# A decoder layer on one core: half two of the tokens first in the output projection, S1 products early, sums of h by token tile

## The chip, the cores and the metric

The kernel runs on one core of a Trainium2 chip. Its engines are TensorE (PE, with its weight loads shown apart as PEld), VectorE (DVE), ScalarE (ACT), GpSimd (POOL) and SyncE (SP), which issues the DMAs. The metric is the device time of one execution, in microseconds.

## The reference

One hybrid decoder layer in float32, 1024 tokens of 1024 channels. The part around the change is its end:

```python
x = x + gate1 * jnp.dot(merged, w_out)                    # output projection
h2 = _rmsnorm(x, norm2_w) * (1.0 + scale2) + shift2
ffn = jnp.dot(jax.nn.silu(jnp.dot(h2, w_ffn_gate)) * jnp.dot(h2, w_ffn_up), w_ffn_down)
x = x + gate2 * ffn                                       # w_ffn_gate, w_ffn_up: 1024 x 2816
```

## The kernel before, in words

Every large product is made in three parts: each factor is split into hi (rounded to fp32r by ACT) and lo (the rest, a subtraction on DVE or POOL), and PE adds hi·hi, hi·lo and lo·hi in one PSUM bank. A 128x512 output block of depth 512 so takes twelve matmuls.

**Output projection** (L1258 to L1315). It runs in two passes over the eight token tiles of 128 tokens, one for each half of the output channels. A tile takes 24 matmuls of 512 columns. In the second pass each tile is then finished: addition to x (L1283), sum of squares (L1284), reciprocal root on POOL (L183), two scalings to `xn` (L1296), eight transposes on PE (L1299), and eight scale-and-shift operations from PSUM to `hraw`, four on ACT (L1305) and four on DVE (L1307). The first matmul of a tile is kept behind the transposes of a tile two or three earlier by an order constraint without a wait (`turns_first`).

**Feed-forward, gate and up.** h is cut in four blocks of 512 channels by 512 tokens: h11 and h21 are the two channel halves of token half one (tiles 0 to 3), h12 and h22 those of half two (tiles 4 to 7). The products follow Winograd's form of Strassen: 256 output columns of one weight matrix (a `Stream`, 22 in all: gate and up for 11 column blocks p) need seven products M1 to M7 of a weight factor by a block or sum of h: M1 with h11, M2 with h21, M4 with h22, M5 with S1 = h12 + h22, M6 with S2 = S1 - h11, M7 with S3 = h11 - h12, M3 with S4 = h21 - S2. The weight factors of M5, M6, M7 and M4 are differences of weight blocks (L743, L747). M1, M6, M7, M4 add up in one bank A (tag `ya`, four buffers), M5 and M3 in B (tag `yb`, two).

Weights come in as `raws`, four buffers of 512 KB, two to a stream; a factor goes through `tmp` (four buffers) to a slot `fhi`/`flo` (five), hi on ACT (L710), lo on POOL (L711).

Before the change the early products are M1 and M2 of streams 0 to 3 (p = 0, 1), 96 matmuls, as they need half one alone, whose split blocks h11 and h21 are put together tile by tile (L1220, L1221, lo on POOL). After the last tile come the sums S1, S2, S3, S4 (four operations of 128x512 each, L1415) and their splits (L1422 on ACT, L1423 on DVE), and with them the remaining five products of the first two streams; then the streams follow one after the other, a factor prepared two products ahead (`run`, `behind`). Split blocks live in seven slabs (`COMBOS`), which are shared with the buffers of the output projection.

The order in which an engine gets its instructions is set when the kernel is compiled, by a scheduler that follows dependencies and priorities; it moves instructions ahead of others of the same engine where they are ready sooner.

Of the kernel before, what the change touches and what calls it, by code (L numbers as in the profile page):

```python
# [43 lines left out]
def tile_hybrid_layer(ctx: ExitStack, tc: tile.TileContext, x, c, w_ada, b_ada, norm1_w, w_in,  # L44
# [659 lines left out]
    EARLY = ["M1", "M2"]  # L704

# [3 lines left out]
    def split_block(src, hi, lo):  # L709
        nc.scalar.activation(hi, src, AF.Copy)  # L710
        nc.gpsimd.tensor_sub(lo, src, f32(hi))  # L711

    class Stream:


        def __init__(self, env, w, c0):
            self.env, self.w, self.c0 = env, w, c0
            self.c, self.ready, self.blocks = {}, {}, {}
            self.early = False
            self.next = None  # L720
# [11 lines left out]
        def prepare(self, m):  # L732
            if m not in self.ready:
                self.open()
                self.ready[m] = self.factor(m)

        def factor(self, m):
# [3 lines left out]
            elif m == "M4":  # L741
                src = self.t2
                nc.vector.tensor_sub(src, b["21"], src)  # L743
            else:
                src = four(self.env.tmp())
                x, y = {"M5": ("12", "11"), "M6": ("22", None), "M7": ("22", "12")}[m]
                nc.vector.tensor_sub(src, b[x], b[y] if y else self.t1)  # L747
# [5 lines left out]
            split_block(src, hi, lo)  # L753
            return hi, lo

        def copy(self, c, ps):
            self.c[c] = self.env.quad(self, c)
            nc.scalar.activation(self.c[c], ps, AF.Copy)
# [4 lines left out]
        def product(self, m, after=None):  # L763
# [3 lines left out]
            hhi, hlo = self.env.side[SIDE[m]]  # L767
            if m == "M1":
                self.A = self.env.a()
            if m == "M5":  # L770
                self.B = self.env.b()
            ps = self.B if m in ("M5", "M3") else self.env.b() if m == "M2" else self.A
            for k in range(4):
                first, last = k == 0 and m in ("M1", "M5", "M2"), k == 3
                mm = nc.tensor.matmul(ps, lhsT=whi[:, k, :], rhs=hhi[:, k, :], start=first, stop=False,  # L775
# [3 lines left out]
                nc.tensor.matmul(ps, lhsT=wlo[:, k, :], rhs=hhi[:, k, :], start=False, stop=last,  # L779
# [7 lines left out]
            if m == "M6":  # L787
                self.copy("12", ps)
            if m == "M3":
# [3 lines left out]
            if m == "M2" and self.early:  # L793
                self.m2 = self.env.quad(self, "m2")
                nc.scalar.activation(self.m2, ps, AF.Copy)
                return
# [19 lines left out]
    class GateEnv:  # L816
        n_q, n_raw = 0, 0

# [371 lines left out]
    COMBOS = {"h11": 3, "h21": 4, "S1": 1, "S2": 0, "h22": 6, "S4": 2, "S3": 5}  # L1190
# [27 lines left out]
    def put_combo(name, o, src):  # L1218
        hi, lo = (c[:, :, o:o + P] for c in combo[name])
        nc.scalar.activation(hi, src, AF.Copy)  # L1220
        nc.gpsimd.tensor_sub(lo, src, f32(hi))  # L1221
# [10 lines left out]

    early_w = {}
    turned = {}
# [5 lines left out]
    early_raw = {}  # L1240

    def early_load(p):
        for u, w in enumerate((w_ffn_gate, w_ffn_up)):
            raw = early_raw[p, u] = raw_pair().rearrange("p (k n) -> p k n", k=KT)
            nc.sync.dma_start(out=raw, in_=w[:, 2 * p * P:(2 * p + 1) * P].rearrange("(k p) n -> p k n", p=P))

    def early_split(p, slots):
        for i, m in enumerate(("M1", "M2")):
            for u in range(2):
                hi, lo = slots(2 * u + i)  # L1250
                split_block(early_raw[p, u][:, 4 * i:4 * i + 4, :], hi, lo)
                early_w[p, u, m] = hi, lo

    def slab_slots(p):
        t = slab_tile((0, 6)[p], [P, 4, 2, H], R, "early")
        return lambda i: (four(t[:, i, 0, :]), four(t[:, i, 1, :]))

    for hf in range(2):  # L1258
# [15 lines left out]
        for t in range(NT):  # L1274
# [16 lines left out]
            if t == 0:  # L1291
                for name in ("h11", "h21"):
                    alloc_combo(name)
            for g in range(2):
# [5 lines left out]
                for i in range(4):  # L1300
# [7 lines left out]
            if th == 0:  # L1308
                put_combo("h11", o, hraw[0][:, 0, :, o:o + P])
                put_combo("h21", o, hraw[0][:, 1, :, o:o + P])  # L1310
            if t == 4:
                early_load(0)
                early_split(0, slab_slots(0))
            if t == 5:
                early_load(1)  # L1315
                early_split(1, slab_slots(1))
# [13 lines left out]
    class FfnEnv:  # L1330
        def __init__(self):
# [5 lines left out]
        def quad(self, st, c):  # L1337
            if st.p < 2 and c == "11":
                return held[:, 2 * st.p + st.u, :]
            if st.p == 1 and c == "m2":  # L1340
# [3 lines left out]
        def use(self, st, c):  # L1344
            if st.u == 0:
                src = st.A if c == "21" else st.c[c]
                if c == "21":
                    st.c[c] = quad_tile("c21")
                nc.scalar.activation(st.c[c], src, AF.Silu)
            else:  # L1350
                a = streams[st.p, 0].c[c]
                nc.vector.tensor_mul(a, a, st.A if c == "21" else st.c[c])
# [58 lines left out]
    def sums(a, b, op):  # L1411
        out = []
        for k in range(4):
            out.append(quad_tile("hs"))
            nc.vector.tensor_tensor(out[k], a[k], b[k], op=op)  # L1415
        return out

    def split_combo(name, srcs, eng):
        alloc_combo(name)
        for k in range(4):  # L1420
            hi, lo = (c[:, k, :] for c in combo[name])
            nc.scalar.activation(hi, srcs[k], AF.Copy)  # L1422
            eng.tensor_sub(lo, srcs[k], f32(hi))  # L1423

    held = ffn.tile([P, 4, H], F32, name="held", tag="dw")
    held2 = const.tile([P, 2, H], F32, name="held2", tag="gate")
    streams = {}
    for p in range(NP):
        for u, w in enumerate((w_ffn_gate, w_ffn_up)):
            st = streams[p, u] = Stream(fenv, w, 2 * p * P)  # L1430
            st.p, st.u = p, u
            st.ready = {m: early_w[p, u, m] for m in EARLY if (p, u, m) in early_w}
            st.early = p < 2
    turns = {(0, 0, "M1"): {0: 6}, (0, 1, "M1"): {2: 7}}
    for p in range(2):
        for m in EARLY:
            for u in range(2):
                streams[p, u].product(m, turns.get((p, u, m)))
    h11, h21, h12, h22 = ([hr[:, g, k, :] for k in range(4)] for hr in hraw for g in range(2))
    s1 = sums(h12, h22, ALU.add)  # L1440
    split_combo("S1", s1, nc.vector)
    s2 = sums(s1, h11, ALU.subtract)
    split_combo("S2", s2, nc.vector)
    for p in range(2):
        for u in range(2):
            streams[p, u].add("11", streams[p, u].m2)
    s3 = sums(h11, h12, ALU.subtract)
    s4 = sums(h21, s2, ALU.subtract)
    split_combo("S4", s4, nc.vector)
    split_combo("h22", h22, nc.vector)  # L1450
    split_combo("S3", s3, nc.vector)
    flow = [streams[p, u] for p in range(NP) for u in range(2)]
    flow[0].open()
    flow[1].open()
    seq = [(st, m) for m in ORDER if m not in EARLY for st in flow[:2]]
    seq += [(st, m) for st in flow[2:] for m in ORDER if not (st.early and m in EARLY)]

# [198 lines left out]
```

## Time and profile before

| | |
|---|---|
| three runs | 1805.69 us median (1802.42 to 1805.93) |
| profiled execution | 1804.04 us, span 1802.3 us |
| mean granted TensorE clock | 0.988 |
| busy: PE, PEld | 1706.0 us (95%), 1397.9 us (78%) |
| busy: DVE, ACT, POOL | 1212.2 (67%), 740.5 (41%), 937.9 us (52%) |
| second pass of the output projection | from 1074.3 us of the span |
| last early product ends | 1147.0 us |

Times in rows are microseconds from the start of the span. A matmul's listed duration overlaps that of its neighbours, so PE's pace is read from starts. A window row gives each engine's busy time and its instructions in the stretch, the granted clock (1.00 is 2.4 GHz, 0.50 is 1.2 GHz), the busy share of the DMA engines and GB/s. In a timeline the bracket at the end of a row is the engine's idle time before it and what ended it.

### The profile page before, as it was taken

How to read it: one execution, taken by the hardware profiler on the slowest of the kernel's cores; microseconds unless marked ns; L12 is line 12 of the kernel's file. 1: busy time of each engine (PE TensorE's matmuls, PEld its weight loads, DVE VectorE, ACT ScalarE, POOL GpSimd, SP SyncE). 2: the span in 40 equal slices, each digit the busy share in tenths (PEclk: the TensorE clock that was granted, in tenths of full speed). 3: DMA queues.
4: the chain of work that ended last, by engine and by line, in shares of the span. 5: the costliest groups of instructions: out<-in, count | busy, mean ns of one | idle time of the engine just before them, and what ended most of it. 6: DMA issues, size and time to landing. Idle time of an engine off the chain costs nothing. (4 is left out here: it accounts for less than half of the span.)

```text
span 1802.3 us, 24616 instructions
## 1 busy us (share of the span) xinstructions
PE 1706.0 (95%) x8266; PEld 1397.9 (78%) x8266; DVE 1212.2 (67%) x2088; ACT 740.5 (41%) x1448; POOL 937.9 (52%) x902
## 2 busy tenths in 40 slices
PE   5898989999979999999999999799998999999998
PEld 4797867878757888788777888577777787788887
DVE  7627599999599345479775647856666554486565
ACT  3525532331444344430576145543333333354444
POOL 4571285682565479430355634444544544576564
PEclk9999999999999999999999999999999999999999
DMA  8521235343424355974843710225666332387663
GB/s 282 172 75 40 83 123 187 93 133 98 128 71 129 103 152 196 282 197 138 195 113 135 244 71 24 71 94 183 239 237 229 108 115 88 107 274 229 185 182 111
DMA packets 184703, 266.49 MB, mean 148 GB/s; under 512 B 13872, under 2 KB 113664, under 8 KB 182144
## 3 DMA queue, kind: packets, MB, share of 16 engines
q1 hardware_dynamic: 184576, 264.91, 46.7%
q8 instruction: 65, 1.06, 0.3%
q14 instruction: 62, 0.51, 0.1%
HBM read 195.39 MB, written 69.47 MB: 147 GB/s over the span
## 5 line engine op out<-in xcount | busy, mean ns | idle before, releaser
L711 POOL TENSOR_TENSOR flo<-tmp,fhi 128x512 fp32r<-128x512 f32 x88 | 131.3, 1494 | 153.1 <-ACT fhi L710 130.7
L80 POOL TENSOR_TENSOR wlo<-wraw,whi 128x512 fp32r<-128x512 f32 (+2 forms) x116 | 142.6, 1241 | 105.2 <-ACT whi L77 97.5
L454 DVE TENSOR_SCALAR_CACHE_REDUCE eq<-score,cand 128x384 uint8<-128x384 f32 (+2 forms) x192 | 180.8, 942 | 4.3
L120 PE MATMUL mm<-whi,hT_hi 128*128 128x512 f32 (+1 forms) x432 | 162.9, 380 | 2.3 <-ACT qk L615 1.8
L123 PE MATMUL mm<-whi,hT_lo 128*128 128x512 f32 (+1 forms) x432 | 163.4, 379 | 0.0
L122 PE MATMUL mm<-wlo,hT_hi 128*128 128x512 f32 (+1 forms) x432 | 162.7, 377 | 0.0
L775 PE MATMUL ya<-hc,fhi 128*128 128x512 f32 x336 | 133.7, 399 | 12.1 <-DVE c L761 10.2
L1504 DVE TENSOR_TENSOR dslot<-draw,dslot 128x512 fp32r<-128x512 f32 x88 | 92.8, 1082 | 68.9 <-ACT dslot L1503 60.2
L777 PE MATMUL ya<-hc,fhi 128*128 128x512 f32 x336 | 132.7, 395 | 5.1 <-DVE hc L1423 5.1
L779 PE MATMUL ya<-hc,flo 128*128 128x512 f32 x336 | 131.2, 394 | 0.0
L1503 ACT ACTIVATE dslot<-draw 128x512 fp32r<-128x512 f32 x154 | 89.8, 626 | 97.3 <-PE ya L1522 36.6
L1504 POOL TENSOR_TENSOR dslot<-draw,dslot 128x512 fp32r<-128x512 f32 x66 | 97.2, 1482 | 62.3 <-ACT dslot L1503 59.7
L711 POOL TENSOR_TENSOR flo<-raws,fhi 128x512 fp32r<-128x512 f32 x58 | 81.2, 1401 | 71.6 <-ACT fhi L710 54.7
L77 ACT ACTIVATE whi<-wraw 128x512 fp32r<-128x512 f32 (+2 forms) x116 | 67.0, 590 | 123.3 <-DMA wraw<-in_w_in_dram 52.2
L775 PE MATMUL yb<-hc,fhi 128*128 128x512 f32 x248 | 98.0, 396 | 5.2 <-ACT hc L1422 3.7
L710 ACT ACTIVATE fhi<-tmp 128x512 fp32r<-128x512 f32 x88 | 55.3, 631 | 115.9 <-PE ya L777 71.2
L779 PE MATMUL yb<-hc,flo 128*128 128x512 f32 x248 | 96.8, 391 | 3.7 <-POOL flo L711 3.7
L777 PE MATMUL yb<-hc,fhi 128*128 128x512 f32 x248 | 96.8, 390 | 1.8 <-DVE hc L1423 1.7
L1070 POOL TENSOR_SCALAR sx<-sx,mx 128x128 f32<-128x128 f32 (+7 forms) x64 | 47.5, 747 | 92.1 <-DVE mx L1069 69.2
L711 POOL TENSOR_TENSOR wlo<-wraw,whi 128x512 fp32r<-128x512 f32 x52 | 79.8, 1544 | 29.0 <-ACT whi L710 24.6
L120 PEld LDWEIGHTS mm<-whi,hT_hi 128*128 128x128 f32 x432 | 82.3, 191 | 14.2 <-ACT qk L615 2.2
L123 PEld LDWEIGHTS mm<-whi,hT_lo 128*128 128x128 f32 x432 | 82.4, 191 | 12.7
(407 smaller groups left out, 4944.3 us busy)
## 6 DMA issues: line engine op xcount, KB each, us to landing
draw<-act_d SPq DMA_DIRECT2D x77, 256.0 KB
mw<-in_w_ada_dram SPq DMA_DIRECT2D x32, 512.0 KB
act_d<-c SPq DMA_DIRECT2D x62, 256.0 KB
raw<-in_w_in_dram SPq DMA_DIRECT2D x26, 512.0 KB
raws<-in_w_ffn_gate_dram SPq DMA_DIRECT2D x24, 512.0 KB
raws<-in_w_ffn_up_dram SPq DMA_DIRECT2D x24, 512.0 KB
dw<-in_w_ffn_down_dram SPq DMA_DIRECT2D x22, 512.0 KB
dw_d<-dw SPq DMA_DIRECT2D x11, 1024.0 KB
```

What stands on the lines that cost most here:

```text
L77: ins = nc.scalar.activation(hi[:, :n], raw[:, :n], AF.Copy)
L80: nc.gpsimd.tensor_sub(lo[:, :n], raw[:, :n], f32(hi[:, :n]))
L120: ins = nc.tensor.matmul(ps, lhsT=ahi, rhs=whi[:, :n], start=(i == 0), stop=False)
L122: nc.tensor.matmul(ps, lhsT=ahi, rhs=wlo[:, :n], start=False, stop=False)
L123: nc.tensor.matmul(ps, lhsT=alo, rhs=whi[:, :n], start=False, stop=(i == last))
L454: ins = [nc.vector.tensor_scalar(eq[:, :sc.shape[1]], sc, thr[j], None, op0=op, op1=ALU.add, accum_out=cnt[:, j:j + 1]) for j, sc in enume ...
L711: nc.gpsimd.tensor_sub(lo, src, f32(hi))
L775: mm = nc.tensor.matmul(ps, lhsT=whi[:, k, :], rhs=hhi[:, k, :], start=first, stop=False, skip_group_check=True)
L777: nc.tensor.matmul(ps, lhsT=whi[:, k, :], rhs=hlo[:, k, :], start=False, stop=False, skip_group_check=True)
L779: nc.tensor.matmul(ps, lhsT=wlo[:, k, :], rhs=hhi[:, k, :], start=False, stop=last, skip_group_check=True)
L1503: nc.scalar.activation(slot[:, 0], raw, AF.Copy)
L1504: lo_eng.tensor_sub(slot[:, 1], raw, f32(slot[:, 0]))
```

## The change

- The second pass takes token tiles in the order 4, 5, 6, 7, 0, 1, 2, 3.
- The sums of h are made tile by tile and in place: a tile of half two splits h22, turns it to S1 (h22 := h12 + h22) and splits that; a tile of half one splits h11 and turns S1 to S2 there; after the last tile h21 is split and turned to S4. All lo parts of these are on DVE. S3 is formed in a tile of its own.
- The early products are M5 of streams 0 to 3 (48 matmuls). Their factor b12 - b11 is formed in pass one. M6 forms that difference again.
- The first two streams then run M1, M2, M4, M6, M3, M7; M4, M3 and M6 end in other banks than before. Factors' lo parts are on DVE until the ninth of these products.
- More scale-and-shift operations go to ACT: six of eight in half two, all eight in half one.
- Slabs are shared in another way (`COMBOS`).

```diff
     def product(self, m, after=None):
+            own = m in ("M1", "M5", "M2") or m == "M3" and "M5" in self.early or m in self.early
             if m == "M1":
-                self.A = self.env.a()
+                ps = self.A = self.env.a()
+            elif own:
+                ps = self.env.b()
+            else:
+                ps = self.B if m == "M3" else self.A
...
-            if m == "M6":
+            if m == "M6" and "M5" in self.early:
+                self.c["12"] = self.env.quad(self, "12")
+                nc.vector.tensor_add(self.c["12"], self.c["22"], ps)
+            elif m == "M6":
                 self.copy("12", ps)
+            if m == "M4" and m in self.early:
+                self.copy("21", ps)
+                return
...
+            if m == "M7" and "M4" in self.early:
+                self.add("21", ps)
+                self.env.use(self, "21")
...
-    COMBOS = {"h11": 3, "h21": 4, "S1": 1, "S2": 0, "h22": 6, "S4": 2, "S3": 5}
+    COMBOS = {"h22": 3, "S1": 4, "h11": 1, "h21": 0, "S2": 6, "S4": 5, "S3": 2}
...
     def put_combo(name, o, src):
         hi, lo = (c[:, :, o:o + P] for c in combo[name])
         nc.scalar.activation(hi, src, AF.Copy)
-        nc.gpsimd.tensor_sub(lo, src, f32(hi))
+        nc.vector.tensor_sub(lo, src, f32(hi))
+
+    def put_half2(o):
+        h11, h21, h12, h22 = parts_of(o)
+        put_combo("h22", o, h22)
+        nc.vector.tensor_add(h22, h12, h22)
+        put_combo("S1", o, h22)
+
+    def put_half1(o):
+        h11, h21, h12, s1 = parts_of(o)
+        put_combo("h11", o, h11)
+        nc.vector.tensor_sub(s1, s1, h11)
+
+    def put_rest(o):
+        h11, h21, h12, s2 = parts_of(o)
+        put_combo("h21", o, h21)
+        nc.vector.tensor_sub(h21, h21, s2)
...
+    def early_factors():
+        slot = slab_tile(6, [P, 4, 2, H], R, "early")
+        for p in range(2):
+            for u, w in enumerate((w_ffn_gate, w_ffn_up)):
+                raw = raw_pair().rearrange("p (k n) -> p k n", k=4)
+                nc.sync.dma_start(out=raw, in_=w[:H, 2 * p * P:(2 * p + 2) * P].rearrange("(k p) n -> p k n", p=P))
+                nc.vector.tensor_sub(raw[:, :, P:], raw[:, :, P:], raw[:, :, :P])
+                early_w[p, u] = four(slot[:, 2 * p + u, 0, :]), four(slot[:, 2 * p + u, 1, :])
+                split_block(raw[:, :, P:], *early_w[p, u])
...
-        for t in range(NT):
+        order = list(range(NT)) if hf == 0 else [4, 5, 6, 7, 0, 1, 2, 3]
+        for n, t in enumerate(order):
...
-                if hf and t > 2:
-                    turns_first(mm, t - (3 if t < 6 else 2))
+                if hf and n > 2:
+                    turns_first(mm, order[n - (3 if n < 6 else 2)])
...
             if hf == 0:
+                if t == 2:
+                    early_factors()
                 continue
...
-                    if g == 0:
-                        nc.scalar.activation(h_to, h_of, AF.Identity, scale=sc, bias=sh)
+                    if k < (6 if n < 4 else 8):
+                        ins = nc.scalar.activation(h_to, h_of, AF.Identity, scale=sc, bias=sh)
...
+            (put_half2 if th else put_half1)(o)
+    alloc_combo("h21")
+    for i in range(4):
+        put_rest(i * P)
...
     class FfnEnv:
+        lo_engine = nc.vector
...
+    tmps = [tmp_tile() for _ in range(2)]
+    fenv.tmp = lambda: tmps.pop(0) if tmps else tmp_tile()
...
+    for st in flow[:2]:
+        st.prepare("M1")
+        turns_after(scaled[3], st.split)
+    s3 = ffn.tile([P, 4, H], F32, name="s3", tag="dw")
+    for st, after in zip(flow, (None, {0: 2}, {2: 3}, {0: 3})):
+        st.product("M5", after)
+        if st.p == 0:
+            turns_after(scaled[3], st.copied)
+    split_combo("S2", hraw[1][:, 1])
+    seq = [(st, m) for m in ("M1", "M2", "M4", "M6", "M3", "M7") for st in flow[:2]]
+    n_first = len(seq)
+    seq += [(st, m) for st in flow[2:] for m in ORDER if m not in st.early]

     def behind(i):
         st, m = seq[i]
-        if st.early and m == "M4":
-            fenv.use(st, "11")
-        if i < 10:
+        if i == 0:
+            for k in range(4):
+                nc.vector.tensor_sub(s3[:, k, :], hraw[0][:, 0, k, :], hraw[1][:, 0, k, :])
+        if i == 1:
+            split_combo("S4", hraw[0][:, 1])
+        if i == 3:
+            split_combo("S3", s3)
+        if i == 8:
+            fenv.lo_engine = nc.gpsimd
+        if i == 9:
+            flow[2].open()
+        if i < n_first:
             return
```

`after` in `st.product("M5", after)` keeps the matmuls of one depth step behind the transposes of a token tile: {2: 3} is depth step 2 behind tile 3, the last one now. `scaled[3]` is the first scale-and-shift of that tile on ACT.

## Rows read from the trace of the kernel before

**Rows 1.** The page's busy line: us, share of the span, instructions

```profile
PE 1706.0 (95%) x8266; PEld 1397.9 (78%) x8266; DVE 1212.2 (67%) x2088; ACT 740.5 (41%) x1448; POOL 937.9 (52%) x902
```

**Rows 2.** Windows of 50 us: length, engines' busy time, clock, DMA share, GB/s

```profile
1150.00:1200.00 50.00, 37.22 (x141) 28.48 (x141) 40.49 (x53) 18.86 (x34) 23.00 (x15) 0.86 0.35 109
1200.00:1250.00 50.00, 48.28 (x213) 39.66 (x212) 25.60 (x32) 18.41 (x32) 24.13 (x18) 1.00 0.43 146
```

**Rows 3.** Windows: second pass up to the hole, and the hole

```profile
1147.10:1179.00 31.90, 19.04 (x59) 12.92 (x59) 29.58 (x37) 13.97 (x27) 15.54 (x9) 0.79 0.37 115
1074.30:1147.10 72.80, 72.80 (x353) 60.49 (x352) 50.03 (x102) 42.20 (x94) 29.89 (x21) 1.00 0.05 15
```

**Rows 4.** Timeline of PE: start, us, engine, line, what, idle before

```profile
1161.49 0.80 PE L777 MATMUL ya<-hc,fhi 128*128 128x512 f32 x1 [5.13 <-DVE hc L1423]
...
1162.52 0.63 PE L775 MATMUL ya<-hc,fhi 128*128 128x512 f32 x1
1162.94 0.63 PE L777 MATMUL ya<-hc,fhi 128*128 128x512 f32 x1
...
1238.10 0.39 PE L777 MATMUL ya<-hc,fhi 128*128 128x512 f32 x1
...
1241.50 0.39 PE L775 MATMUL yb<-hc,fhi 128*128 128x512 f32 x1
```

**Rows 5.** Waits from 1000 to 1260: total us, times, longest

```profile
PE ya L777 <- DVE hc L1423: 5.1, 1, 5.1
...
PE yb L775 <- ACT hc L1422: 3.7, 1, 3.7
```

**Rows 6.** DVE in the hole: a window, two groups, three timeline rows

```profile
1137.00:1176.00 39.00, 26.14 (x96) 18.62 (x95) 36.67 (x50) 23.57 (x45) 22.94 (x9) 0.86 0.26 82
...
L1423 DVE TENSOR_TENSOR hc<-hs,hc 128x512 fp32r<-128x512 f32 x16 | 12.3, 814 | 0.0
...
L1415 DVE TENSOR_TENSOR hs<-hraw 128x512 f32<-128x512 f32 x4 | 2.5, 686 | 0.0
...
1152.84 1.71 POOL L711 TENSOR_TENSOR flo<-raws,fhi 128x512 fp32r<-128x512 f32 x1
...
1153.35 1.75 DVE L1423 TENSOR_TENSOR hc<-hs,hc 128x512 fp32r<-128x512 f32 x1
...
1174.51 4.89 DVE L1423 TENSOR_TENSOR hc<-hs,hc 128x512 fp32r<-128x512 f32 x8
```

**Rows 7.** Timeline around the last token tile, four engines

```profile
1126.59 0.69 DVE L1283 TENSOR_TENSOR x<-x,ya 128x512 f32<-128x512 f32 x1 [4.09 <-PE ya L123]
...
1130.24 0.89 DVE L1296 TENSOR_SCALAR xn<-x,rstd 128x512 f32<-128x512 f32 x2 [0.73 <-POOL rstd L183]
...
1135.02 1.03 PE L1299 MATMUL ty<-ident,xn 128*128 128x128 f32 x8
1135.65 1.50 ACT L1305 ACTIVATE hraw<-ty,modr 128x128 f32<-128x128 f32 x4 [6.52 <-PE ty L1299]
1135.81 0.48 PE L775 MATMUL ya<-hc,early 128*128 128x512 f32 x1
1136.09 1.37 DVE L1307 TENSOR_SCALAR hraw<-ty,modr 128x128 f32<-128x128 f32 x4 [4.96 <-PE ty L1299]
```

**Rows 8.** Groups of the second pass on DVE, 1074 to 1136

```profile
L1214 DVE TENSOR_TENSOR mlo<-merged,mhi 128x512 fp32r<-128x512 f32 x13 | 11.6, 891 | 1.9 <-ACT mhi L1213 1.9
...
L1296 DVE TENSOR_SCALAR xn<-x,rstd 128x512 f32<-128x512 f32 x16 | 9.4, 629 | 4.7 <-POOL rstd L183 4.7
...
L1288 DVE TENSOR_TENSOR s<-ssum 128x1 f32<-128x1 f32 x8 | 3.2, 395 | 1.7 <-ACT ya L1284 1.7
```

**Rows 9.** Early loads, DVE before pass one, DMA in one window

```profile
L1245 SPq DMA_DIRECT2D raws<-in_w_ffn_gate_dram x2: 384/2513/4642, 997.5 to 998.8; - x2
...
1036.35 0.85 DVE L1214 TENSOR_TENSOR mlo<-merged,mhi 128x512 fp32r<-128x512 f32 x1 [3.06 <-ACT mhi L1213]
...
1190.00:1195.00 5.00, 5.00 (x23) 4.14 (x23) 2.39 (x3) 2.24 (x4) 3.25 (x3) 1.00 0.60 182
```

More of the change, by code (lines that the diff above doesn't have):

```diff
@@ L767, in product @@
             hhi, hlo = self.env.side[SIDE[m]]
+            own = m in ("M1", "M5", "M2") or m == "M3" and "M5" in self.early or m in self.early
             if m == "M1":
[L769 removed]
+                ps = self.A = self.env.a()
[3 more added lines that the diff above has]
+                ps = self.B if m == "M3" else self.A
             if m == "M5":
[L771 to L772 removed]
+                self.B = ps
             for k in range(4):
[L774 to L775 removed]
+                mm = nc.tensor.matmul(ps, lhsT=whi[:, k, :], rhs=hhi[:, k, :], start=own and k == 0, stop=False,
                                       skip_group_check=True)
@@ L778, in product @@
                                  skip_group_check=True)
-                nc.tensor.matmul(ps, lhsT=wlo[:, k, :], rhs=hhi[:, k, :], start=False, stop=last,
+                nc.tensor.matmul(ps, lhsT=wlo[:, k, :], rhs=hhi[:, k, :], start=False, stop=k == 3,
                                  skip_group_check=True)
@@ L1230, in raw_pair @@
         return raws[0][:, n_raw[0] % 4, :]
-    early_w = {}
-    turned = {}
+    turned, scaled = {}, {}
     def turns_first(ins, t):
         turns_after(ins, turned[t])
[L1240 to L1256, printed above, removed]
+    early_w = {}
+    def early_factors():
[7 more added lines that the diff above has]
+                split_block(raw[:, :, P:], *early_w[p, u])
     for hf in range(2):
@@ L1290, in tile_hybrid_layer @@
             th, o = t // 4, (t % 4) * P
-            if t == 0:
-                for name in ("h11", "h21"):
-                    alloc_combo(name)
+            if n == 0:
+                alloc_combo("h22")
+                alloc_combo("S1")
+            if n == 4:
+                alloc_combo("h11")
             for g in range(2):
@@ L1337, in quad @@
         def quad(self, st, c):
-            if st.p < 2 and c == "11":
-                return held[:, 2 * st.p + st.u, :]
-            if st.p == 1 and c == "m2":
+            if st.p == 1 and c == "22":
                 return held2[:, st.u, :]
@@ L1409, in down_sums, with split_combo @@
         todo.insert(4, lambda: nc.sync.dma_start(out=dw_d[p], in_=dws[p]))
[L1411 to L1418, printed above, removed]
+    def split_combo(name, srcs):
         alloc_combo(name)
@@ L1431, in tile_hybrid_layer @@
             st.p, st.u = p, u
[L1432 to L1451, printed above, removed]
-    flow = [streams[p, u] for p in range(NP) for u in range(2)]
-    flow[0].open()
-    flow[1].open()
-    seq = [(st, m) for m in ORDER if m not in EARLY for st in flow[:2]]
@@ L1456, in tile_hybrid_layer @@
-    seq += [(st, m) for st in flow[2:] for m in ORDER if not (st.early and m in EARLY)]
+            if p < 2:
+                st.early = ("M5",) if p else ("M5", "M4")
+                st.ready["M5"] = early_w[p, u]
+    flow = [streams[p, u] for p in range(NP) for u in range(2)]
+    for st in flow[:2]:
+        st.prepare("M1")
+        turns_after(scaled[3], st.split)
+    s3 = ffn.tile([P, 4, H], F32, name="s3", tag="dw")
+    held2 = const.tile([P, 2, H], F32, name="held2", tag="gate")
+    for st, after in zip(flow, (None, {0: 2}, {2: 3}, {0: 3})):
+        st.product("M5", after)
+        if st.p == 0:
+            turns_after(scaled[3], st.copied)
```

49 lines of the change are left out of this document (22 added, 27 removed).

## The prediction

> **What bounds the kernel now.** I read the page's engine line first: PE is busy 95% of the span [rows 1], so only time in which PE waits or runs slowly can be won, as the change removes no matmul on the way to the output: seven products of twelve matmuls for each of the 22 weight streams stay. Second, busy time by stretches of 50 us around the changed lines [rows 2]: 1200 to 1250 has PE at 48.28, 1150 to 1200 only at 37.22 with a granted clock of 0.86. Third, that stretch alone [rows 3]: from 1147.10 to 1179.00 only 59 matmuls started. The 72.80 us before it were dense.
>
> The price of the hole comes from the pitch of back-to-back matmuls: from 1238.10 to 1241.50 fifteen of them start, 0.227 us each [rows 4]. 59 of them need 13.4 us; they took 31.9. **The hole costs 18.5 us.** A part of it is clock: after a wait of 5.13 us the matmuls stand 0.43 us apart instead of 0.227 [rows 4].
>
> Fourth, the waits of PE in that neighbourhood [rows 5]: the longest end on `hc` written by DVE at L1423 and by ACT at L1422, the split sums S1, S2, S4 of h. Fifth, DVE itself [rows 6]: 36.67 of the 39 us from 1137 on, so it is the engine that the sums queue on. The groups of that stretch show the work: 16 lo parts of sums at L1423, four times four sums at L1415 (one group of them shown), and between them the factors of the first weights. Alone, a 128x512 two-input operation takes 0.68 us, and eight in a row take 4.89, so 0.61 each; single ones that run beside a POOL subtraction take 1.75, the subtraction 1.71 [rows 6]. The cause is order: S1 = h12 + h22 can't start before the last token tile, though it needs half two alone, and the 96 early matmuls (M1 and M2 of four streams) run out at 1147.0.
>
> **The change part by part.** *Tokens 4 to 7 first.* Each tile keeps 24 matmuls and eight transposes (6.2 us of PE: 24 x 0.227, and 0.79 from the transposes' start at 1135.02 to the next matmul [rows 7]), and the order constraints keep their distance. Nothing is won or lost by this itself; it makes h12, h22 and so S1 complete four tiles before the end.
>
> *Sums and splits by tile, in place.* A tile of half two gets on DVE the lo of h22, the sum, and the lo of S1; one of half one the lo of h11 and a difference. POOL loses its eight lo parts here, DVE gains. For a half-two tile DVE then has, by the means of the present pass [rows 8] and the addition of 0.69 [rows 7], 2 x 0.89 + 0.69 + 0.40 + 2 x 0.63 + 2 x 0.34 (four take 1.37 [rows 7]) + 3 x 0.68 = 6.9 us against 6.2 of PE; with 0.61 for each 128x512 operation it is 5.5. So the bounds are 0 and 4 x 0.7 = 2.8 us; below zero is excluded, since PE is dense there already. I take 0: the half-one tiles need only 5.5 by the same means, the early products add 10.9 us of PE that nothing in DVE must feed, and POOL, the cause of the long means, is nearly idle then. ACT gets six or eight of a tile's scalings (four take 1.50 [rows 7]) where it has four; it was busy 42.2 of 72.8 us [rows 3].
>
> *Early factors.* Four subtractions (b12 - b11) and four splits for M5 replace eight splits for M1 and M2. Their four loads are the same 512 KB each that SP issued from 997.5 on [rows 9]; no queue is passed. The subtractions (4 x 0.68) fit DVE's idle 3.06 us before its first lo part of the pass [rows 9]; without that cover they cost 2.7. POOL still makes four lo parts in pass one, none in pass two. Zero.
>
> *Early products.* 48 matmuls, 10.9 us, instead of 21.8. They must cover what the last tile leaves open. Now the addition that follows the last tile's matmuls starts at 1126.59, and the normalised rows are ready at 1131.13, by square, power and scaling: 4.5 us, 4.7 with the 0.2 from the last matmul [rows 7]. The written order puts one product and half of another (4.1 us) and the previous tile's transposes (0.8) there, so 0 exposed. Behind the last transposes stand 18 matmuls, 4.1 us, in which ACT does eight scalings (two rows like the 1.50 one, started 0.6 after the transposes) and the hi of h11, and DVE the lo: 0.6 + 2.8 + 0.6 + 0.7 = 4.7, against 0.8 + 4.1 = 4.9. M1 can start; call this moment 0. The splits of M1's factors, put ahead of the scalings on ACT, lie in ACT's 6.52 us idle [rows 7].
>
> *The first group behind it.* Order M1, M2, M4, M6, M3, M7 for two streams: 12 products, 32.6 us. From the last transposes to M7 DVE has: lo parts of h11, h21 (1 tile each), S2, S4, S3 (4 each), 14; sums 6; factor differences 8 (M6 forms M5's again: four of them); lo parts of factors 9, now on DVE; additions of results 8. That is 45 x 0.61 = 27.5 us, against 36.7 of PE. The total fits; the deadlines decide. In the order of the code DVE reaches the factor of the first M4 at 13.1 (h21's and S2's share 4.1, M2's two lo parts 1.2, s3 2.4, S4 2.4, then M6's and M4's factor 3.0), behind which its bank is freed by M2's addition at 13.7; M4 is due at 10.9. That is 2.8, and its second stream waits 1.0 more: 3.8. If M6's and M4's differences are done while DVE waits for the last tile (gaps of 4.09 and 4.96 us now [rows 7], and raw weights loaded long before), it is 0. I take 2, the middle. New waits on slabs: S2's split waits until the early products have read theirs, S4's until S2's split and s3 are done, S3's behind S4; behind each the next DVE additions queue, which is the same 3.8.
>
> *Later.* Stream three's first factor needs a raw buffer that M7's differences free, by 24 us in that order; its load of 512 KB at the 182 GB/s of [rows 9] takes an estimated 2.9, split 0.6 + 1.3, so ready at 29 against 32.6. Covered by 4 us. Copies and additions of the held results fall away on ACT and DVE, off the path: nothing.
>
> **Sum.** 18.5 - 2 = 16.5 saved. The profiled execution took 1804.04 us (span 1802.3), so 1787.5. It stands 1.65 under the median of the runs, 1805.69: **1789**.
>
> One rule of the notes speaks against moving lo parts from POOL to DVE: the Trainium skill, Perfetto Trace Analysis, Optimizing Scalar/DVE Operations, has work of a saturated DVE handed to ScalarE or GpSimd, and adds that between DVE and GpSimd it might not help, since they share a read port. By its first half the sum would end in the third rival below, by its second in the forecast; the 0.68 and 1.75 us of [rows 6] lean to the second.
>
> **The rivals.** *DVE keeps its order and its slowness.* For: the mean lo part was 0.81 us in the hole [rows 6], and every deadline goes by DVE. Then the 13.7 becomes 18.5, M4 waits 7.6 and 1.3, and eight matmuls run at 0.43, 1.6 more: 10.5. Against: POOL has next to nothing beside it. 1804.04 - 18.5 + 10.5 + 1.65 = 1798.
>
> *Given back at the next streams.* If M7's differences slip by 8 us, the 4 us of cover are gone and some 3.5 to 4 are given back at the third stream: 1793. For: the four raw buffers are all held by the first two streams; against: they only need two short operations.
>
> *Slower: DVE becomes the bound of the first group.* If all 45 operations take the 1.75 us of those beside POOL, they need 78.8 us against 36.7, a hole of 42: 1804 + 42 - 18.5 + 1.65, about 1829. It breaks even at (36.7 + 18.5) / 45 = 1.23 us each. Against: POOL is given factors only from the ninth product on, and the eight in a row of [rows 6] ran at 0.61.
>
> *It doesn't do what it says.* If S1 comes so late in DVE's queue that no early product runs before the last tile's transposes, the 4.7 us of the last chain stand bare, and the 2.8 of the tiles' bound add to it: 1789 + 7.5 = 1797.
>
> **How the numbers follow.** Forecast 0.69, own range 1785 to 1793 (a residue of 0 to 3.8, and up to 2 us of shift in the stretches after 1200, where PE still waits 1.7 of 50 us [rows 2]); first rival 0.15, given back 0.06, slower 0.06, late S1 0.04. From 0.2% (3.6 us), about what can be told from no change, all but the slow one and a third of the first rival, which may end nearer the old time, are faster: 0.89; within 0.05; slower 0.06. The range 1784 to 1798 holds the forecast, two rivals and most of the first.
>
> **What would show it.** Right: granted clock 1.00 throughout 1130 to 1180, no wait of PE on `hc` above 2 us, M1's first matmul some 5 us behind the last transposes, DVE below 85% in the first group with 0.68 us operations, everything later some 16 us earlier. Wrong: a wait of PE at an early product or at M4's factor above 4 us; DVE operations of 1.7 us in the first group; a new wait of the third stream on its load; or a later stage that ends as late as now.

## The result, and the profile after

The changed kernel takes 1794.77 us (median; 1792.51 to 1796.41) where the kernel before takes 1805.28 in runs beside it: a ratio of 0.9944, 95% interval 0.9927 to 0.9961. It is faster. 10.5 us are saved where 16.5 were forecast: the time lies in the wide range of 1784 to 1798, which holds two of the rivals too, but 1.8 us above the forecast's own range of 1785 to 1793. The profiled execution took 1796.41 us (span 1794.6). Executions of one kernel differ by 0.2 to 0.7% (the twelve runs of e0 below go from 1790.56 to 1802.93), already ahead of the changed lines: the second pass of this one starts 4.0 us later than in the trace of before, over unchanged code. So moments of two traces are compared from the first matmul of the second pass on, and by work done: "product n" is the feed-forward product that has n products of twelve matmuls before it.

First the page's busy line of the changed kernel, answering to [rows 1]:

```profile
PE 1703.6 (95%) x8266; PEld 1399.4 (78%) x8266; DVE 1211.1 (67%) x2093; ACT 747.4 (42%) x1466; POOL 891.7 (50%) x883
```

The work is the same; POOL has lost 46 us and 19 instructions. Then the windows (columns as in [rows 2]): three of 50 us, the first group of products by itself (from the first M1 to the end of M7), and four short ones:

```profile
1100.00:1150.00 50.00, 46.87 (x222) 38.26 (x221) 41.95 (x84) 38.52 (x91) 2.75 (x5) 0.97 0.07 22
1150.00:1200.00 50.00, 48.13 (x212) 39.20 (x210) 43.17 (x61) 21.78 (x37) 17.18 (x12) 1.00 0.60 202
1200.00:1250.00 50.00, 48.13 (x205) 39.33 (x206) 31.36 (x40) 17.50 (x31) 23.96 (x17) 0.97 0.62 219
...
1145.24:1178.18 32.94, 32.93 (x145) 26.95 (x144) 30.94 (x46) 19.10 (x33) 7.03 (x5) 1.00 0.42 135
...
1135.00:1140.00 5.00, 1.97 (x6) 1.63 (x7) 5.00 (x10) 5.00 (x13) 0.00 (x0) 0.88 0.01 3
1140.00:1145.00 5.00, 5.00 (x18) 3.94 (x18) 5.00 (x9) 3.05 (x6) 0.00 (x0) 0.78 0.65 208
...
1200.00:1205.00 5.00, 4.28 (x13) 3.44 (x14) 1.96 (x4) 1.22 (x3) 1.27 (x1) 0.66 0.60 242
...
1278.00:1283.00 5.00, 3.19 (x15) 2.41 (x14) 3.25 (x4) 1.82 (x4) 1.99 (x2) 1.00 0.52 212
```

The stretch from 1150 to 1200, with PE at 37.22 in [rows 2], is now at 48.13: the hole is gone. Two smaller losses stand where there were none, at 1135 to 1145 and at 1200 to 1205, each with a clock below 1.00. The timeline of PE (columns as in [rows 4]) shows both; the last three rows are a shorter gap further on:

```profile
1133.64 0.39 PE L789 MATMUL yb<-hc,early 128*128 128x512 f32 x1
1133.88 1.03 PE L1336 MATMUL ty<-ident,xn 128*128 128x128 f32 x8
1138.03 0.50 PE L785 MATMUL yb<-hc,early 128*128 128x512 f32 x1 [3.12 <-ACT c L765]
...
1139.27 0.63 PE L787 MATMUL yb<-hc,early 128*128 128x512 f32 x1
1139.70 0.63 PE L789 MATMUL yb<-hc,early 128*128 128x512 f32 x1
...
1142.25 0.39 PE L789 MATMUL yb<-hc,early 128*128 128x512 f32 x1
...
1145.24 0.61 PE L785 MATMUL ya<-hc,fhi 128*128 128x512 f32 x2
...
1197.81 0.39 PE L787 MATMUL yb<-hc,fhi 128*128 128x512 f32 x1
1200.72 0.80 PE L785 MATMUL ya<-hc,fhi 128*128 128x512 f32 x1 [2.53 <-DVE held L768]
...
1203.79 0.40 PE L787 MATMUL ya<-hc,fhi 128*128 128x512 f32 x1
...
1277.90 0.39 PE L785 MATMUL yb<-hc,fhi 128*128 128x512 f32 x1
1280.10 0.50 PE L785 MATMUL ya<-hc,fhi 128*128 128x512 f32 x1 [1.81 <-DVE c L768]
1280.44 0.40 PE L787 MATMUL ya<-hc,fhi 128*128 128x512 f32 x1
```

First loss: behind the last transposes (1133.88) the third early product waits 3.12 us for ACT's copy of the first one (L765), which frees its bank; then eight matmuls stand some 0.43 us apart. All 24 matmuls of the third and fourth early product stand behind the transposes. M1 starts at 1145.24, 11.4 us after the transposes' start and 10.3 after their end. Second loss: the last product of stream three, M4, waits for a DVE addition that reads the bank in which M4 goes on adding (M4, and not an M1 as the expectations below have it: ACT reads the finished bank for M4's silu at 1205.46, right behind these twelve matmuls). A longer wait of this kind stands later, 4.04 us at 1304.78; the kernel before has one of 4.84 us at 1370.18. Of the waits on `hc` in [rows 5] none is left: from 1100 to 1400 PE waits for no slab of h.

How far each kernel has come, in us from the first matmul of its second pass to the start of product n (worked out by counting matmuls in each trace; "end" is the last gate or up matmul; the kernels in the lower rows are those of the experiments; 34 matmuls of the down projection, 7.7 us, stand ahead of "end" in every row but e7's, where none does):

```
                              n=4     14      20      26      70      end
before                       61.8   108.0   124.3   140.6   267.9   518.3
after                        66.9    94.4   110.7   131.7   265.5   507.2
after, run again (e0)        66.9    94.4   110.7   131.7   266.4   508.3
e1  other banks              65.0    97.8   114.1   135.3   266.0   507.9
e2  scalings on DVE          64.2    98.5   114.9   137.0   273.0   515.0
e3  down sums later          68.2    95.7   112.0   128.3   250.7   492.6
e4  down sums in own pair    66.6    94.1   110.5   127.0   251.3   493.1
e5  transposes earlier       63.9    91.0   107.4   128.0   265.4   507.1
e6  e4 and e5                63.8    91.0   107.4   125.2   249.6   491.3
e7  before, without sums     61.8    89.0   105.3   122.6   249.5   494.0
e8  before, down sums        61.8   109.4   125.7   142.1   265.7   507.5
e9  factors' lo on POOL      66.6    99.9   118.0   137.9   266.8   508.6
e10 h's lo on POOL           69.7    97.8   114.5   134.9   275.4   517.2
```

Product 14 stands behind the hole of before. There the change is 13.6 us ahead (108.0 against 94.4), at product 70 only 2.5, at the end 11.1. So two things are to be explained: why 13.6 and not 16.5 at product 14, and why gains come and go behind it.

### The profile page after: what moved, and what is told of

It reads as the page before. It is cut to its first block, busy times and chain, and to the rows that moved or that the text cites. A ratio compares the mean times of both kernels' runs of the same rounds, so it can differ in the third digit from the quotient of the medians.

```text
span 1794.6 us, 24639 instructions
## 1 busy us (share of the span) xinstructions
PE 1703.6 (95%) x8266; PEld 1399.4 (78%) x8266; DVE 1211.1 (67%) x2093; ACT 747.4 (42%) x1466; POOL 891.7 (50%) x883
## 5 line engine op out<-in xcount | busy, mean ns | idle before, releaser
L709 POOL TENSOR_TENSOR flo<-tmp,fhi 128x512 fp32r<-128x512 f32 x79 | 105.1, 1331 | 156.8 <-ACT fhi L708 130.5
L785 PE MATMUL ya<-hc,fhi 128*128 128x512 f32 x344 | 136.1, 396 | 12.1 <-DVE c L768 8.6
L787 PE MATMUL ya<-hc,fhi 128*128 128x512 f32 x344 | 135.0, 392 | 0.0
L785 PE MATMUL yb<-hc,fhi 128*128 128x512 f32 x256 | 100.4, 392 | 0.2
L787 PE MATMUL yb<-hc,fhi 128*128 128x512 f32 x256 | 99.7, 389 | 0.0
```

The source lines that it names most:

```text
L709: (eng or nc.gpsimd).tensor_sub(lo, src, f32(hi))
L787: nc.tensor.matmul(ps, lhsT=whi[:, k, :], rhs=hlo[:, k, :], start=False, stop=False, skip_group_check=True)
```

## The experiments

Every kernel is the changed one with the edit shown, but e7 and e8, which edit the kernel before. The changed kernel itself ran again beside e1 to e3:

> The changed kernel once more, beside its variants on one chip. Expected: 1794 to 1796 us, 10 to 11 us under the kernel before. Its trace should show the two late places again: PE waiting about 3 us at the third early product for ACT's copies of the first two, and about 2.5 us at an M1 for an addition to the held result on DVE, which stands behind differences of the down weights. If one of them is gone in this execution, it was chance and not order.

Measured: 1795.39 us, ratio 0.9958 (0.9944 to 0.9971), and a trace within 1.1 us of the first one's row at every column above. That is how far two traces of one kernel agree. The kernel before took 1803.28 beside it, so here the change is worth 7.9 us and not the 10 to 11 expected; over both sets of runs its worth by medians is 8 to 10.5 us.

### What was the hole worth? (e7)

```
-    s1 = sums(h12, h22, ALU.add)
-    split_combo("S1", s1, nc.vector)
...
+    for to, of in (("S1", "h11"), ("S2", "h21"), ("S4", "h11"), ("S3", "h11"), ("h22", "h21")):
+        combo[to] = combo[of]
```

This leaves out the sums of h and all five splits (S1, S2, S4, h22, S3); the products read the slabs of h11 and h21 in their place.

> The kernel before with the four sums of h and the splits of S1, S2, S4, S3 and h22 left out: the products take the split blocks h11 and h21 in their place, so the output is another one. What is left is the same number of matmuls. It prices the hole: if the sums and splits behind the last tile make all of it, PE has no wait of over 1.5 us between 1147 and 1179 and the time falls by 17 to 19 us, to 1785 to 1787; if the factors of the weights on POOL make a part of it, 5 us or more of waiting stay there.

Measured: 1790.5 us (0.9919, 0.9895 to 0.9942). Product 14 comes at 89.0, dense behind product 8 (72.7 + 72 x 0.227 = 89.0), and 19.0 us before that of the kernel before. So the hole is made by the sums and their splits and costs 19.0, where the prediction read 18.5; of these the change keeps 5.4 (94.4 - 89.0). The time falls by 15.4 us and not by the expected 17 to 19: later stretches give some back here too (18.4 us ahead at product 70).

### What makes the third early product wait? (e1, e2, e5)

ACT's timeline of the changed kernel around the last token tiles:

```profile
1130.87 2.90 ACT L1342 ACTIVATE hraw<-ty,modr 128x128 f32<-128x128 f32 x8 [1.31 <-PE ty L1336]
1133.62 1.19 ACT L1236 ACTIVATE hc<-hraw 128x512 fp32r<-128x512 f32 x2
1134.95 1.50 ACT L1342 ACTIVATE hraw<-ty,modr 128x128 f32<-128x128 f32 x4
1136.33 1.16 ACT L708 ACTIVATE fhi<-raws 128x512 fp32r<-128x512 f32 x2
1137.37 1.09 ACT L765 ACTIVATE c<-yb 128x512 f32<-128x512 f32 x2
1138.33 1.53 ACT L1342 ACTIVATE hraw<-ty,modr 128x128 f32<-128x128 f32 x4
```

ACT works without a pause from 1130.87 to 1142.4, and the two copies that free the early products' banks (1137.37) come behind four of the last tile's scalings (1134.95) and M1's two splits. The code orders splits and copies ahead of `scaled[3]`, but that holds only the scaling of k = 0; four scalings slipped ahead, those of the other channel half (e2 below, which takes these off ACT, has none left there). One theory: the banks are the limit, so other banks remove the loss. The rival: ACT's and DVE's work of the stretch is the limit, and the wait moves. e1 gives the second pair's early products the other two banks:

```
+            elif m == "M5" and self.early == ("M5",):
+                ps = self.env.a()
```

> The changed kernel with M5 of streams three and four in two of the four banks of tag ya, so that these early products need no bank that ACT has yet to copy out. Theory (the two yb banks and the place of the copies in ACT's queue): the wait of 3.1 us and the half clock behind it go, the product group behind it starts about 4 us earlier, 1790 to 1792. Rival (ACT has more work than the stretch has time, whatever the banks): the wait only moves to the first M1, which needs the split of h11 behind the same ACT queue, and the time falls by less than 1.5 us.

Measured: 1793.7 us (0.9947, 0.9928 to 0.9965). M1 starts 1.9 us earlier, but product 14 comes 3.4 later. Its waits from 1100 to 1200 (us in total, times, longest):

```profile
PE yb L787 <- ACT hc L1238: 3.0, 1, 3.0
...
PE yb L789 <- DVE hc L1239: 1.7, 1, 1.7
```

The wait has gone from the copies to the splits of h, as the rival has it; the time alone, 1.7 us under e0's, can't tell the two apart. e2 takes the channel half that slipped ahead off ACT:

```
-                    if k < (6 if n < 4 else 8):
+                    if k < (6 if n < 4 else 4):
```

> The changed kernel with four of the eight scale-and-shift operations of half-one tiles back on DVE, as before. Theory (ACT's queue is full between the last two tiles): two times 1.4 us leave ACT ahead of the copies, which come 2 to 3 us earlier; PE's wait of 3.1 us falls below 1, and the time by 2 to 4 us, to 1791 to 1793. Rival (the copies are late because their target overlaps a buffer that the last transposes still read): the copies stay behind the last transposes, the wait shrinks by less than 1 us, and so does the time.

Measured: 1801.17 us (0.9988, 0.9974 to 1.0002), 5.8 above the changed kernel beside it. Half of the expectation holds: the copies run at 1129.54, ahead of the last transposes (1129.96), the third early product no longer waits for them, and M1 starts 2.7 earlier. So the rival of this run, a buffer that the transposes still read, is out. But now DVE is late: PE waits 1.35 us for it ahead of the last transposes, and more in the first group:

```profile
PE yb L787 <- DVE hc L1237: 4.2, 2, 3.7
```

Product 14 comes 4.1 us later than in the changed kernel. In this stretch DVE has no room either: it is busy for 5.00 of 5 us in both windows from 1135 to 1145 above. e5 leaves the engines their work and lets it begin earlier. The normalised rows of the last tile are ready at 1131.55 (the end of L1333 on DVE), its transposes start at 1133.88, as they are written behind early products:

```
-    for st, after in zip(flow, (None, {0: 2}, {2: 3}, {0: 3})):
+    for st, after in zip(flow, ({1: 2}, {1: 3}, {0: 3}, {0: 3})):
```

> The changed kernel with the last two tiles' transposes a product earlier on PE: most of the first and second early product stands behind them. Theory (ACT and DVE idle between 1126 and 1131 because the transposes stand behind early products, and are full afterwards): the wait at the third early product shrinks from 3.1 to under 1.5 us, the half clock behind it goes, and product 14 starts 3 to 5 us earlier after the start of the second pass; 1790 to 1792. Rival (the sum of ACT's and DVE's work behind the last tile is the bound): the wait reappears at the first group, product 14 moves by less than 1.5 us.

Measured: 1794.21 us (0.9935, 0.9916 to 0.9954). The wait of 3.12 us at the third early product becomes 1.22, and product 14 comes 3.4 earlier, at 91.0, which leaves 2.0 of the hole. The expected time of 1790 to 1792 is missed. At the end of gate and up nothing of the 3.4 is left (507.1 against 507.2): it was given back behind, a part of it here, where from 1100 to 1250 PE waits 4.5 us in place of 2.5:

```profile
PE ya L785 <- DVE held L768: 4.5, 2, 3.3
```

### Who takes the gains back? (e3, e4, e8)

DVE's timeline of the changed kernel ahead of that second loss:

```profile
1192.50 0.67 DVE L768 TENSOR_TENSOR c<-c,yb 128x512 f32<-128x512 f32 x1
1196.38 1.46 DVE L1434 TENSOR_TENSOR dw<-dw 128x512 f32<-128x512 f32 x1 [3.21 <-DMA dw<-in_w_ffn_down_dram]
1198.18 0.69 DVE L1434 TENSOR_TENSOR dw<-dw 128x512 f32<-128x512 f32 x1 [0.34 <-DMA dw<-in_w_ffn_down_dram]
1198.79 0.69 DVE L754 TENSOR_TENSOR tmp<-raws 128x512 f32<-128x512 f32 x1
1199.39 0.68 DVE L1434 TENSOR_TENSOR dw<-dw 128x512 f32<-128x512 f32 x1
1199.99 0.68 DVE L768 TENSOR_TENSOR held<-held,ya 128x512 f32<-128x512 f32 x1
```

DVE is idle for 3.21 us in front of a difference of the down projection's weights (L1434) that waits for its load; the addition that frees the bank for PE (1199.99) stands behind it in the queue. There is one `dw` buffer, so load, differences, store and the next load form a chain, and each link makes DVE wait in order. Waits of the changed kernel from 1150 to 1590:

```profile
DVE dw L1434 <- DMA dw<-in_w_ffn_down_dram: 28.7, 16, 4.3
...
PE ya L785 <- DVE held L768: 2.5, 1, 2.5
```

of the kernel before, in the same stretch:

```profile
DVE dw L1400 <- DMA dw<-in_w_ffn_down_dram: 40.0, 15, 5.5
```

So these waits are not new with the change. But there the first of these differences ran at 1239.0, behind the held results that shared the buffer; with those gone it runs at 1164.6 (78 us earlier, counted from the second pass's start), and the chain reaches into the streams right behind the first group. The last of the 44 differences runs at 1384.9 in the kernel before and at 1319.8 in the changed one. So at product 70 (1342.2 and 1343.8) the changed kernel has all the chain's waits behind it and the kernel before still its longest ahead (4.84 us, at 1370.18): that is, for the most part, why the lead is 2.5 us there and 11.1 at the end. Theory: the differences in DVE's queue take the gains; rival: PE's later gaps have causes of their own. e3 orders each of them behind the last multiplication of the newest pair of streams:

```
-            todo.insert(n[0], lambda: nc.vector.tensor_sub(*(dws[p][:, i, :] for i in (to, x, y))))
+            todo.insert(n[0], lambda: turns_after(nc.vector.tensor_sub(*(dws[p][:, i, :] for i in (to, x, y))),
+                                                  last_mul[-1]))
```

where `last_mul` collects the multiplications that end a pair.

> The changed kernel with the differences of the down weights kept on DVE behind the last multiplication of the stream pair that they belong to, so that DVE does not sit at a load that was only just issued. Theory (an addition that frees a bank stands behind a difference that waits for its load): the wait of 2.5 us at the M1 near 1200 and the half clock behind it go, 3.5 to 4.5 us, and perhaps the similar wait near 1300 as well; 1787 to 1791. Rival (DVE simply has too much to do there, or the wait is for another reason): the wait stays, or comes back at the next pair; change within 1 us.

Measured: 1791.05 us (0.9933, 0.9916 to 0.9951). Of PE's gaps over 1 us only the one at the early products is left, and gate and up end 14.6 us earlier. But the newest pair comes later than needed: three rounds of load, differences and store are left for the end, and in the trace the down projection gives it all back: from the last gate or up matmul to the end it takes 224.5 us against 209.1. Its waits from 1540 to 1792:

```profile
PE yb L1555 <- ACT dslot L1537: 7.7, 1, 7.7
...
PE ya L1555 <- ACT dslot L1537: 1.5, 1, 1.5
```

e4 is the same with `last_mul[p]`, the pair's own:

> The changed kernel with the differences of the down weights of column block p behind the last multiplication of the same block, two blocks earlier than in the run before, so that only one load, sum and store is left at the end of gate and up. Theory (differences ahead of their loads held back additions that free banks): gate and up has no wait of PE above 1.5 us behind the first group, as in the run before, and its last matmul comes about 14 us earlier after the start of the second pass than in the changed kernel; this time nothing is given back in the down projection: 1780 to 1784. Rival (the late differences were only a shift: what DVE does not do there it must do at the end): the down projection waits again and the time stays above 1789.

Measured: **1776.78 us** (0.9849, 0.9825 to 0.9874), 18 below the changed kernel by the medians and 3 below the expected range. From 1150 to 1590 no wait of DVE for `dw` is listed any more, gate and up end 14.1 us earlier, and one wait of PE over 1.5 us is left behind the first group (1.6). e8 puts this same constraint into the kernel before:

> The kernel before, with nothing of the change, only the differences of the down weights put behind the last multiplication of their own column block. Theory (the differences stood ahead of their loads before the change as well, and their chain of load, sum and store paced gate and up in both kernels): the waits of PE from 1240 to 1365, 12.4 us together, go; the last matmul of gate and up comes 11 to 14 us earlier after the start of the second pass; 1790 to 1794. Rival (the change itself brought that by setting the buffer free early): less than 3 us.

Measured: 1791.62 us (0.9924, 0.9902 to 0.9947). Gate and up end 10.8 us earlier, just short of the expected 11, with the hole still in place (product 14 at 109.4). DVE's wait, from 1150 to 1590:

```profile
DVE dw L1403 <- DMA dw<-in_w_ffn_down_dram: 5.0, 2, 2.9
```

With the differences in order on both sides, the change is worth 1791.62 - 1776.78 = 14.8 us by the medians and 507.5 - 493.1 = 14.4 to the end of gate and up in the traces; without, 7.9 to 10.5 and 11.1. What the chain takes is read from the traces, from product 14 to the end of gate and up: the kernel before needs 410.3 us there and the changed one 412.8, so 2.5 are given back; with the order it is 398.1 (e8) and 399.0 (e4). So the chain costs both kernels 12 to 14 us. All the kernels without the order that share the changed kernel's code behind the first group need 408.7 (e9) to 419.5 (e10) there, those with it (e3, e4, e6) 396.9 to 400.3. What the chain leaves of a gain made ahead of it so hangs on the moment at which that gain arrives, and a give-back of 2.5 us lies inside this spread.

### Do lo parts belong on DVE? (e9, e10)

The prediction's durations rest on POOL having next to nothing beside DVE. e9 gives the factors' lo parts of the first group back to POOL (`lo_engine = None`, and the switch to POOL at the ninth product removed), e10 the lo parts of h in the token tiles:

```
-        nc.vector.tensor_sub(lo, src, f32(hi))
+        nc.gpsimd.tensor_sub(lo, src, f32(hi))
```

> The changed kernel with the lo parts of all weight factors on POOL from the first, as before the change. By the reading of the profile that led the prediction (DVE and POOL slow one another, 1.75 against 0.68 us) product 20 after the start of the second pass comes 3 to 8 us later than in the changed kernel. Rival (DVE is full in the first group, so nine operations less on it help): product 20 comes 2 to 4 us earlier.

Measured: 1800.2 us (0.9968, 0.995 to 0.9985); product 20 comes 7.3 us later than in the changed kernel, of which 1.4 are left at the end of gate and up.

> The changed kernel with the lo parts of h22, S1, h11 and h21 by tile on POOL. If moving them to DVE mattered, the early products or the first group come late by 2 to 6 us (POOL takes about 1.5 us for one where DVE takes 0.68, and S1's second split stands behind the first). If DVE's 16 lo parts were what made it late behind the last tile, product 14 comes up to 3 us earlier. If they were covered by PE either way, product 14 moves by less than 1 us.

Measured: 1801.47 us (0.9977, 0.9959 to 0.9995); product 14 comes 3.4 us later, the end of gate and up 10. Both intervals overlap that of the changed kernel, so the places in the traces carry this, not the times. Groups of DVE (columns: what, count, busy us, mean ns, idle before), first the changed kernel from 1130 to 1165:

```profile
L1450 DVE TENSOR_TENSOR hc<-hraw,hc 128x512 fp32r<-128x512 f32 x8 | 5.1, 683 | 0.0
...
L1483 DVE TENSOR_TENSOR s<-hraw,hraw 128x512 f32<-128x512 f32 x4 | 2.6, 684 | 0.0
...
L754 DVE TENSOR_TENSOR tmp<-raws,tmp 128x512 f32<-128x512 f32 x3 | 2.0, 683 | 0.0
```

then e9 from 1130 to 1175, DVE and POOL:

```profile
L1450 DVE TENSOR_TENSOR hc<-hraw,hc 128x512 fp32r<-128x512 f32 x8 | 6.8, 901 | 1.7 <-ACT hc L1449 1.7
...
L1483 DVE TENSOR_TENSOR s<-hraw,hraw 128x512 f32<-128x512 f32 x4 | 3.7, 953 | 0.0
L754 DVE TENSOR_TENSOR tmp<-raws,tmp 128x512 f32<-128x512 f32 x2 | 3.5, 1770 | 0.0
...
L709 POOL TENSOR_TENSOR flo<-raws,fhi 128x512 fp32r<-128x512 f32 x6 | 9.4, 1579 | 6.6 <-ACT fhi L708 6.6
```

The same operations take 901, 953 and 1770 ns where POOL subtracts beside them, and 683 without. The Trainium skill, SBUF — State Buffer, Who interferes with whom, says that a DVE instruction with both inputs in SBUF contends with a GpSimd instruction that reads SBUF; these rows agree.

### Both (e6)

The edits of e4 and e5 together.

> The two edits together. If each works on a wait of its own they add: 1776 to 1780, 25 us or more under the kernel before. If both only move the same work on DVE about, the sum is no better than the better one alone, 1780 to 1784.

Measured: **1775.56 us** (0.9831, 0.981 to 0.9851), span 1774.9. It beats both kernels, by 29.7 and 19.2 us of the first runs' medians (30.3 against the kernel before in runs beside it). Product 14 comes at 91.0 and gate and up end at 491.3, 16 us ahead of the changed kernel. Whether e5's part still counts is not settled: e4 and e6 differ by 1.2 us in medians and 1.8 in the traces, and their intervals overlap. What is left at the early products, in e6's timeline of PE:

```profile
1130.56 0.39 PE L789 MATMUL yb<-hc,early 128*128 128x512 f32 x1
1132.17 0.50 PE L785 MATMUL yb<-hc,early 128*128 128x512 f32 x1 [1.22 <-ACT c L765]
1132.50 0.40 PE L787 MATMUL yb<-hc,early 128*128 128x512 f32 x1
```

## Why the prediction was right, and where it was wrong

**Right: the hole, its price and its cause.** "The hole costs 18.5 us" is 19.0 by e7, which takes its cause away. The price came from the pitch of [rows 4] and the count of [rows 3], so the clock's share was in it.

**Right: DVE's speed.** The first group runs at 0.68 us an operation, where a lo part took 0.81 in the hole of [rows 6], and e9 and e10 show both the contention and that PE pays for it. The rivals by which DVE keeps its slowness or becomes the bound are out for that reason, and the one of the late S1 too: early products run from 1121.17 on, ahead of the last transposes. DVE is much fuller than "below 85%" (30.94 of the 32.94 us of the first group, and 5.00 of 5 in the two windows above), yet it keeps its deadlines: from product 4 to 14 PE needs 27.5 us, where 120 matmuls at 0.227 make 27.2. The sums by tile cost nothing in the second pass, as forecast: PE has no wait there before 1134. (One bound was summed wrongly: a half-two tile with 0.61 for each 128x512 operation needs 6.0 us, not 5.5; that is still below PE's 6.2.)

**Wrong: the residue, by 3.4 us and in its place.** I took 2 us at M4's factor, with bounds of 0 and 3.8. Nothing is lost there; 5.4 are lost ahead of it, at the early products. What I wrote of the chain up to the last transposes, "0 exposed", came true: the rows are ready at 1131.55, and the transposes follow the second early product at 1133.88 without a wait. The steps that failed are the sum behind them, "0.6 + 2.8 + 0.6 + 0.7 = 4.7, against 0.8 + 4.1 = 4.9. M1 can start", and, of the splits on ACT, "lie in ACT's 6.52 us idle". That sum gives ACT the last tile's eight scalings and one split; left out are the previous tile's eight scalings, its splits, M1's splits and the copies, all in ACT's one queue: from 1130.87 to 1142.4 ACT never rests, and the copies come out at 1137.37. That four early products share two banks, and so that a copy has to come between, did not enter my sum at all. By e1 other banks only move the wait; by e5 an earlier start of the transposes leaves 2.0 of the 5.4, and nothing comes up at M4's factor in its place (27.2 us from product 4 to 14). Whether M4 would wait if M1 came as early as forecast, no run shows. That M6's differences would run while DVE waits for the last tile failed too: the first stands at 1134.93, behind the last transposes:

```profile
1134.32 0.69 DVE L1237 TENSOR_TENSOR hc<-hraw,hc 128x512 fp32r<-128x512 f32 x1 [1.22 <-ACT hc L1236]
1134.93 0.68 DVE L753 TENSOR_TENSOR tmp<-raws 128x512 f32<-128x512 f32 x1
```

**Wrong: "Later … off the path: nothing".** In the traces 2.5 us were given back from product 14 to the end of gate and up, as in my second rival, but by another resource: not the raw buffers and stream three's load (no such wait above 2.1 us from 1100 to 1400), but DVE's queue behind the differences of down weights. The cause stood in the trace of before, in a row I did not read: 40.0 us of DVE idle in front of L1400. I had noted that the held results go and counted only their copies and additions; the buffer that they free lets the chain of `dw` start 78 us earlier. That the chain holds gate and up back in both kernels, by 12 to 14 us, is shown by e4 and e8. That starting earlier is what makes it cost the changed kernel 2.5 us more is argued: with the order 0.9 are left, which two traces of one kernel differ by as well, and the change moves the whole stretch too.

**Together.** 19.0 - 5.4 - 2.5 makes 11.1 in the traces, against 10.5 and 7.9 by the medians; the rest is within the spread of executions. Both misses point the same way, so nothing cancelled by luck. The time alone would not have told this from two of the rivals (1797 and 1793); the traces do. Besides DVE's share, the signs that I named for it came out so: a clock of 1.00 from 1130 to 1180 is wrong (0.88 and 0.78); no wait of PE on `hc` above 2 us is right, but only as the wait stood on `c`; M1 some 5 us behind the last transposes is wrong (11.4, counted from their start as the forecast did); everything 16 us earlier is wrong (13.6, then 2.5, then 11.1). Of the signs against it, the wait at an early product stayed below the 4 us that I had named (3.12).

## What to carry to other kernels

A gain in one stage arrives at the end only if no queue behind it is paced by something else: before pricing a change, look for long waits of an engine on a DMA in the stages that follow, even where that engine is not the bound, and name what stands behind them in its queue. When a stall is filled with other work, add up every engine's queue through the filled stretch, copies that free banks included, not only the chain of data. And an order constraint on one instruction of a group does not hold the others.

## What was not expected of the hardware

What a wait of PE cost beyond itself. After the wait of 3.12 us (behind eight transposes) eight matmuls stood some 0.43 us apart, the pitch of the lower clock (1.2 GHz), with a granted clock of 0.78 from 1140 to 1145. From 1138.03 to 1142.25 eleven steps took 4.2 us where 11 x 0.227 make 2.5: 1.7 more. After the wait of 2.53 us seven steps, from 1200.72 to 1203.79, took 3.1 in place of 1.6: 1.5 more, with 0.66 from 1200 to 1205. After 1.81 us (ahead of 1280.10) the next step took 0.34, the one behind it 0.23 again, and the window shows 1.00. This is read from these waits alone; no run varied their length.
